# A streaming encoder layer on one core: high and low part of the sample as one stationary operand, squares of the attention's norm split in two, ten attention rows instead of eight

## The chip, the core and the metric

The kernel runs on one core of a Trainium2 chip. The metric is device time in microseconds, the median of several executions; smaller is better. The core has a matrix engine (TensorE, PE in the profile, its weight loads PEld), three engines for elementwise work (DVE = VectorE, ACT = ScalarE, POOL = GpSimd) and a queue that issues all transfers (SP). They run side by side and wait for each other through semaphores.

## What is computed

One layer of an encoder with two branches, for two inputs: a prompt of 2048 frames and a sample of 64 frames that continues a stream of 4096 past frames. All is float32. Cut to what matters:

```
h = rmsnorm(x, norm_g) @ w_in                    # 1024 -> 6144 columns
qa, ka, va, za, qb, kb, vb, zb, ga, gb = split(h)
qa, ka = rmsnorm over 64 (qa, qn_g), (ka, kn_g)
oa = diff_attention(qa, ka, va)                  # (softmax_1 - lam * softmax_2) @ v, 4 heads, v of 128
ob, state = retention(qb, kb, vb)                # 4 heads of 128, with decay
oa = rmsnorm(oa, subln_g) * 0.8 * silu(za)
ob = rmsnorm(ob) * silu(zb)
m  = sigmoid(ga + b0) * (oa @ w_oa) + sigmoid(gb + b1) * (ob @ w_ob)
y  = x + m @ w_out
```

The prompt and the sample share the weights. Outputs are y, k, v and the retention state of both.

## The kernel before

**Split products.** [...] To keep precision, each operand is held as two fp32r parts: a high part (a rounding copy, by ACT) and a low part (the difference, by DVE or POOL). A product of two such operands is three products: high by high, high by low, low by high. In `mm_group` (line 491) these are the three entries of `ops`, with the 128 input features of a step `c` as contraction, 8 steps in all. A product of plain float32 operands, as in `rms_t` (line 812), is one call that the profile shows as two records.

**Projections.** x is normalised, transposed on TensorE and split into `xh`, `xl` (`x_tile`, line 369). Columns of w_in arrive in pieces (`w_load`) and are split on ACT and POOL (`w_split`, `w_piece`, `w_low`). The columns q, k and v of the attention and v of the retention are computed with frames as rows of the result (`natural`, line 587, and `opening`, line 510, for the very first group): x is the stationary operand, 128 frames at a time, and w the moving one, 512 or 256 columns wide. The sample's 64 frames are the ninth tile of half 0 and use 64 stationary columns. After each group of products one of three finishers is spawned (`fin_qk` line 616, `fin_va` line 696, `fin_vb` line 733); it reads the accumulation bank "mm" with ACT and DVE, gives the bank back and stores its results in DRAM scratch. The other columns are computed with w as stationary operand (`transposed`, line 749), where the sample is 64 more moving columns.

**Attention.** For a pair of 128-query blocks `qk_block` (line 926) makes scores in banks "s", DVE moves them out with the position bias into a "row" (128 x 1024 float32), ACT takes exponentials there, and `at_pv` (line 1012) transposes the rows and multiplies by v into the one bank "pv". Of rows there are ROWS = 8 (line 32). `rms_t` (line 794) normalises the result, 33 times in all: squares on ACT, a float32 product by a matrix of 1/128 that sums them over partitions into bank "tp", logarithm and exponential on ACT, a correction step on DVE and POOL.

**Output.** `out_stream` (line 1645) makes, for each of 8 groups of 256 prompt frames (plus 8 sample frames each, 264 columns), 8 tiles of m (`m_tile`, `m_fin`), and from them two tiles of y of 128 frames (`y_tile`, line 1598, and `y_fin`). The sample's columns of m are collected in two tiles `ms`, and its own y tile of 64 rows comes last of all.

**What sets the order.** The kernel writes the instructions of PE, ACT and DVE in a fixed order. A planner does it while the program is built: each stage is a generator (a task with a priority), `loop` (line 86) runs the first task by priority whose wake time has come by PE's estimated clock, and `P`, `A`, `V`, `G` and `ld` (from line 119) add estimated durations. `take` waits for a free buffer of a kind (the numbers are in BUFS, line 33), `give` returns it with a time. So projections, which have the lowest priority, fill the time in which attention waits. On the chip the order is fixed and only semaphores decide the times. All transfers go in order through SP's queue.

## Time and profile before

| | |
|---|---|
| three runs, us | 2001.48, 2004.52, 2001.47; median 2001.48 |
| the profiled execution, us | 2002.83 |
| its span in the trace, us | 2001.0 |
| granted TensorE clock, mean | 0.999 |
| TensorE instructions recorded | 12402 |
| DMA: moved, share of the 16 engines' time | 281 MB, 47.2% on the one queue that carries the data |
| first TensorE product, us from the span's start | 1.05 |

How to read it: the profile is of one execution, with times in microseconds from the start of the span. A line names the source line (L500), the engine, the operation, what it writes and reads by the program's tile names (`mm<-wh,xh`), and its shape; "128\*64" on a product is contraction by stationary columns and "128x512" the moving operand. In brackets stands how long the engine was idle before and what ended that. Names in a pair of read tiles are not in the order of the call. Where tasks interleave, one line of code stands for many groups, so a stage is read by its stretch of time.

### The profile page before, as it was taken

The numbers are of one execution on the slowest core, as the hardware profiler recorded it, in microseconds if no ns is written. First come the engines' busy times: TensorE is split into PE (matmuls) and PEld (weight loads), VectorE is DVE, ScalarE is ACT, GpSimd is POOL, SyncE is SP. The second block draws the span as 40 slices with busy tenths as digits, with TensorE's granted clock in tenths as the row PEclk, the third lists the DMA queues.
The fourth block names the chain that finished last, engine by engine and source line by source line (L and its number), as shares of the span: only waits on it lengthen the run. The fifth ranks groups of instructions, "written<-read, shape, count | busy, mean of one in ns | idle before, by whom it ended". The sixth has DMA issues, their size and how long they took to land.

```text
span 2001.0 us, 34243 instructions
## 1 busy us (share of the span) xinstructions
PE 1985.4 (99%) x12402; PEld 1780.0 (89%) x12402; DVE 992.0 (50%) x2665; ACT 958.6 (48%) x2096; POOL 414.8 (21%) x383
## 2 busy tenths in 40 slices
PE   9999999999999999999999999999999999999999
PEld 7778999999998999999999888888888898889997
DVE  6453666553331421546866555644653457444432
ACT  6432676654442433535766655644654555333330
POOL 2310211211112221221211121221112434222210
PEclk9999999999999999999999999999999999999999
DMA  7646454344565463563353252372233676444431
GB/s 242 202 144 181 131 163 121 105 144 139 158 173 132 136 177 107 160 198 127 110 152 100 75 161 77 106 204 90 74 98 106 203 222 194 152 129 142 135 92 53
DMA packets 330269, 280.96 MB, mean 140 GB/s; under 512 B 64690, under 2 KB 296114, under 8 KB 330099
## 3 DMA queue, kind: packets, MB, share of 16 engines
q1 hardware_dynamic: 330098, 278.77, 47.2%
q8 instruction: 98, 1.61, 0.4%
q14 instruction: 73, 0.59, 0.1%
HBM read 187.19 MB, written 91.49 MB: 139 GB/s over the span
## 4 chain that ended last, share of the span: by engine, by line
PE 95%; DVE 2%; DMA 1%; ACT 1%; issue 0%; SPq 0%; POOL 0%; ACTq 0%; POOLq 0%
PE mm L500 53%; PE s L944 3%; PE s L945 3%; PE at L1624 3%; PE at L1051 3%; PE at L1625 3%; PE at L1626 3%; PE pv L1031 2%; PE pv L1030 2%; PE pv L1029 2%; PE mm L1556 2%; PE mm L1558 2%; PE mm L1557 2%; PE s L1558 2%; PE s L1557 2%; PE s L1556 2%
## 5 line engine op out<-in xcount | busy, mean ns | idle before, releaser
L500 PE MATMUL mm<-xh,wh 128*128 128x512 f32 (+2 forms) x1280 | 461.2, 360 | 0.0
L500 PE MATMUL mm<-xh,wl 128*128 128x512 f32 (+2 forms) x1280 | 451.7, 353 | 0.0
L500 PE MATMUL mm<-xl,wh 128*128 128x512 f32 (+2 forms) x1280 | 450.9, 352 | 0.0
L472 POOL TENSOR_TENSOR wl<-ws,wh 128x512 fp32r<-128x512 f32 x189 | 250.0, 1335 | 906.3 <-ACT wh L462 642.3
L500 PE MATMUL mm<-wh,xh 128*128 128x256 f32 (+3 forms) x864 | 272.1, 315 | 0.5 <-DVE tlo L713 0.3
L500 PEld LDWEIGHTS mm<-xh,wl 128*128 128x128 f32 x1280 | 240.9, 188 | 32.0
L500 PEld LDWEIGHTS mm<-xh,wh 128*128 128x128 f32 x1280 | 241.2, 188 | 29.7 <-issue 0.2
L500 PEld LDWEIGHTS mm<-xl,wh 128*128 128x128 f32 x1280 | 241.4, 189 | 29.0
L500 PE MATMUL mm<-wh,xl 128*128 128x256 f32 (+3 forms) x864 | 266.9, 309 | 0.1
L500 PE MATMUL mm<-wl,xh 128*128 128x256 f32 (+3 forms) x864 | 266.5, 308 | 0.0
L770 ACT COPY ev<-mm 128x512 f32<-128x512 f32 x140 | 71.4, 510 | 241.7 <-PE mm L500 223.1
L500 PEld LDWEIGHTS mm<-wh,xh 128*128 128x128 f32 (+1 forms) x864 | 162.2, 188 | 11.5 <-ACT xh L388 0.6
L500 PEld LDWEIGHTS mm<-wl,xh 128*128 128x128 f32 (+1 forms) x864 | 162.4, 188 | 10.5
L500 PEld LDWEIGHTS mm<-wh,xl 128*128 128x128 f32 (+1 forms) x864 | 162.2, 188 | 10.6 <-DVE xl L389 0.6
L1066 DVE TENSOR_TENSOR atl<-at,ath 128x512 fp32r<-128x512 f32 (+1 forms) x144 | 93.7, 659 | 140.7 <-ACT ath L1064 140.6
L983 ACT ACTIVATE row<-row,a_mx 128x1024 f32<-128x1024 f32 (+7 forms) x160 | 153.5, 963 | 16.6 <-DVE a_mx L963 16.4
L953 DVE CUSTOM_DVE_ANT_0 row<-s,dfar 128x512 f32<-128x512 f32 (+2 forms) x192 | 117.8, 631 | 73.0 <-PE s L945 71.8
L462 ACT CAST wh<-ws 128x512 fp32r<-128x512 f32 x192 | 116.5, 618 | 40.7 <-PE mm L500 28.0
L1064 ACT CAST ath<-at 128x512 fp32r<-128x512 f32 (+1 forms) x144 | 79.5, 563 | 98.9 <-PE at L1051 96.6
L944 PE MATMUL s<-K,q 128*128 128x512 f32 (+3 forms) x320 | 120.2, 381 | 2.5 <-DVE a_acc L953 2.5
L945 PE MATMUL s<-K,q 128*128 128x512 f32 (+3 forms) x320 | 115.4, 362 | 0.0
L1004 DVE SCALAR_TENSOR_TENSOR row<-row,a_w 128x1024 f32<-128x1024 f32 (+4 forms) x96 | 98.1, 1031 | 26.7 <-ACT row L1001 26.5
(207 smaller groups left out, 3943.6 us busy)
## 6 DMA issues: line engine op xcount, KB each, us to landing
ws<-in_w_in_dram SPq DMA_DIRECT2D x192, 256.0 KB, 3.1
q<-qT SPq DMA_DIRECT2D x128, 128.0 KB, 3.0
V<-vN SPq DMA_DIRECT2D x24, 512.0 KB, 5.1
K<-kT SPq DMA_DIRECT2D x48, 256.0 KB, 4.3
gt<-gaT SPq DMA_DIRECT2D x64, 132.0 KB, 2.1
gt<-gbT SPq DMA_DIRECT2D x64, 132.0 KB, 2.2
xt<-in_x_prompt_dram SPq DMA_DIRECT2D x16, 512.0 KB, 6.0
kn<-in_cache_k_T_dram SPq DMA_DIRECT2D x32, 256.0 KB, 4.0
```

The source lines that it names most:

```text
L462: self.nc.scalar.copy(h, st)
L472: self.nc.gpsimd.tensor_sub(l, st, h.bitcast(F32))
L500: nc.tensor.matmul(ps, p, q, start=c == 0 and i == 0, stop=c == KC - 1 and i == 2)
L944: nc.tensor.matmul(ps, q1s, kk, start=True, stop=False)
L945: nc.tensor.matmul(ps, q2s, kk, start=False, stop=True)
L953: nc.vector.tensor_tensor_reduce(out=units[k0 // 1024][:, k0 % 1024:k0 % 1024 + n], in0=ps, in1=tab, scale=-SLOPES[h], scalar=3.0e38, op0= ...
L983: nc.scalar.activation(u, u, AF.Exp, bias=mx, scale=-1.0, accum_out=lp[:, k:k + 1])
L1004: nc.vector.scalar_tensor_tensor(out=u0, in0=u0, scalar=w[:, 0:1], in1=u1, op0=ALU.mult, op1=ALU.add)
L1066: nc.vector.tensor_sub(al[:, :w], at[:, :w], ah[:, :w].bitcast(F32))
L1556: nc.tensor.matmul(ps, wh[:, csl], oh, start=kt == 0, stop=False)
L1557: nc.tensor.matmul(ps, wh[:, csl], ol, start=False, stop=False)
L1558: nc.tensor.matmul(ps, wl[:, csl], oh, start=False, stop=kt == 3)
```

## The change

- The sample's high and low part are copied by GpSimd, when the sample's tile is transposed, into a tile `xs` of 128 columns (64 high, 64 low).
- In `mm_group`, where the result has 64 rows, a step makes two products instead of three: `xs` by the high part of w, into 128 rows of the bank (rows 0 to 63 high by high, rows 64 to 127 low by high), and `xh` by the low part of w, into rows 0 to 63.
- The two halves of the bank then have to be added. `halves` copies all 128 rows out (ACT), a transfer moves rows 64 to 127 to partitions 0 to 63, DVE adds, and the old finisher runs from that buffer instead of from the bank.
- `y_tile` does the same for the sample's y, with `ms` as one tile of 128 columns and `y_halves` as its end. The sample's y tile now stands between the last two prompt tiles, and takes its buffers from the kind "wst" instead of "xt" and "yt".
- In `rms_t`, the copy out of the bank goes first; squares are then taken from the copy, once in float32 and once rounded to fp32r, DVE makes the difference, and the sum over partitions is two fp32r products by the matrix of ones instead of one float32 product.
- ROWS goes from 8 to 10, and the scratch that the program reserves for dynamic DMA is set to 1024 bytes per partition, which makes room.

```diff
-ROWS = 8
+ROWS = 10
@@ x_tile
             self.give(tag, t2)
+            if r == 64:
+                for k, part in enumerate((hi, lo)):
+                    nc.gpsimd.tensor_copy(self.xs[:, 4 * q:4 * q + 4, 64 * k:64 * k + 64], part)
+                    t2 = self.G(256, t2)
@@ mm_group
+            if ps.shape[0] == 64:
+                pair = [(ps, xh, b), (both, self.xs[:, c, :], a)]
+                for i, (o, p, q) in enumerate(pair if c else pair[::-1]):
+                    nc.tensor.matmul(o, p, q, start=c == 0 and i == 0, stop=c == KC - 1 and i == 1)
+                    self.P(n)
+                ops = ()
@@ natural, opening
-            self.spawn(fin(ps[:r, :n * len(group)], r, len(group), t0, self.pe + LAT), 0, "w")
+            self.spawn_fin(fin, ps, r, n * len(group), len(group), t0)
+    def spawn_fin(self, fin, ps, r, n, nu, t0):
+        t = self.pe + LAT
+        done = fin(ps[:r, :n], r, nu, t0, t) if r == 128 else self.halves(ps[:, :n], n, t, fin, t0)
+        self.spawn(done, 0, "w")
+
+    def halves(self, ps, n, t, fin, t0):
+        yield from self.take("ev")
+        up = self.sb(self.ep, [128, 512], "ev", "up")[:, :n]
+        self.nc.scalar.copy(up, ps)
+        t = self.A(n, t)
+        self.give("mm", t)
+        yield t
+        yield from self.take("tlo")
+        dn = self.sb(self.ep, [128, 512], "tlo", "dn")[0:64, :n]
+        t = self.ld(dn, up[64:128], 256 * n)
+        yield t
+        self.nc.vector.tensor_add(up[0:64], up[0:64], dn)
+        t = self.V(n, t)
+        self.give("tlo", t)
+        yield from fin(up[0:64], 64, 1, t0, t, "ev")
@@ rms_t
-        nc.scalar.activation(sq, ps, AF.Square)
-        t1 = self.A(n, t)
         nc.scalar.copy(o, ps)
         t2 = self.A(n, t)
         self.give(tag, t2)
+        nc.scalar.activation(sq, o, AF.Square)
+        self.A(n, t)
+        nc.scalar.activation(hi, o, AF.Square)
+        t1 = self.A(n, t)
         yield t1
+        nc.vector.tensor_sub(lo, sq, hi.bitcast(F32))
+        t = self.V(n, t1)
+        yield t
         yield from self.take("tp")
         mb = self.psum("tp")[:, :n]
-        nc.tensor.matmul(mb, self.ones, sq, start=True, stop=True)
-        t = self.P(4 * n)
+        nc.tensor.matmul(mb, self.ones_r, hi, start=True, stop=False)
+        nc.tensor.matmul(mb, self.ones_r, lo, start=False, stop=True)
+        self.P(n)
+        t = self.P(n)
@@ y_tile
+            if sel is None:
+                pair = [(ps[:64], self.ms[:, ct, 0], wl[:, nsl]), (ps, self.ms[:, ct], wh[:, nsl])]
+                for i, (o, m, w) in enumerate(pair if ct else pair[::-1]):
+                    nc.tensor.matmul(o, m, w, start=ct == 0 and i == 0, stop=ct == 7 and i == 1)
+                    t = self.P(512)
+    def y_halves(self, ps, xt, y, r, t):
+        nc = self.nc
+        yield from self.take("wst")
+        yt = self.sb(self.z4, [128, 512], "wst", "oyt")
+        yield t
+        nc.vector.tensor_copy(yt[64:128], ps[64:128])
+        t2 = self.V(512, t)
+        nc.vector.tensor_add(xt, ps[0:64], xt)
+        t = self.V(512, t)
+        self.give("at", t)
+        yield t2
+        t2 = self.ld(yt[0:64], yt[64:128], 1 << 17)
+        yield t2
+        nc.vector.tensor_add(yt[0:64], yt[0:64], xt)
+        t = self.V(512, max(t, t2))
+        self.give("wst", t)
+        yield t
+        self.give("wst", self.st(y, yt[0:64], 2048 * r))
@@ out_stream
             for tt in range(2):
+                if g == 7 and tt:
+                    yield from self.y_tile(7, None, 64, self.i["x_sample"][0], self.o["y_sample"][0])
...
-        yield from self.y_tile(7, None, 64, self.i["x_sample"][0], self.o["y_sample"][0])
@@ kernel
-    nc = _bacc.Bacc("TRN2", target_bir_lowering=False, num_devices=1)
+    nc = _bacc.Bacc("TRN2", target_bir_lowering=False, num_devices=1, dynamic_dma_scratch_size=1024)
```

More of the change, by code (lines that the diff above doesn't have):

```diff
@@ L29 @@
 NEAR0 = 384
-ROWS = 8
+ROWS = 10
 BUFS = {"thi": 1, "tlo": 2, "ev": 3, "q": 2, "K": 4, "V": 4, "ath": 2, "atl": 2,
-        "ws": 3, "w": 12, "r_o": 1, "r_sq": 1, "r_y": 1, "state": 2,
+        "ws": 3, "w": 12, "r_o": 1, "r_sq": 1, "r_y": 1, "r_hi": 1, "r_lo": 1, "state": 2,
         "mm": 2, "s": 2, "at": 2, "pv": 1, "tp": 1,
@@ L493, in mm_group @@
         seg, xsl = x
+        if ps.shape[0] == 64:
+            both = self.both
         for c in range(KC):
@@ L498, in mm_group @@
             ops = ((a, xh), (a, xl), (b, xh)) if wfirst else ((xh, a), (xh, b), (xl, a))
+            if ps.shape[0] == 64:
+                pair = [(ps, xh, b), (both, self.xs[:, c, :], a)]
[3 more added lines that the diff above has]
+                ops = ()
             for i, (p, q) in enumerate(ops):
@@ L516, in opening @@
         self.x_alloc(1)
+        self.xs = self.xp.tile([128, KC, 128], F32R, tag="xs", name="xs")
         us, low = [], []
@@ L579, in opening @@
             yield from self.take("mm")
-            ps = self.psum("mm")
+            ps = self.both = self.psum("mm")
             self.until(self.xt_ready[j])
@@ L583, in opening @@
                                      j == 8, between)
-            self.spawn(fin(ps[:r], r, 1, 128 * j if j < 8 else T, self.pe + LAT), 0, "w")
+            self.spawn_fin(fin, ps, r, 512, 1, 128 * j if j < 8 else T)
             yield self.pe
@@ L601, in natural @@
                     yield self.xt_ready[j0 + u]
+                self.both = ps[:, :n]
                 yield from self.mm_group(ps[:r, n * u:n * u + n], n, us, slice(0, n),
@@ L619, in fin_qk, with fin @@
         hs = slice(2 * g, 2 * g + nh)
-        def fin(ps, r, nu, t0, t):
+        def fin(ps, r, nu, t0, t, bank="mm"):
             n, ng, rt = 128 * nh * nu, 2 * nh * nu, r * nu
@@ L637, in fin @@
                 t2 = self.V(n, t)
-            self.give("mm", max(t1, t2))
+            self.give(bank, max(t1, t2))
             yield t1
@@ L699, in fin_va, with fin @@
         hs = slice(2 * g, 2 * g + nh)
-        def fin(ps, r, nu, t0, t):
+        def fin(ps, r, nu, t0, t, bank="mm"):
             n, rt = 128 * nh * nu, r * nu
@@ L714, in fin @@
             t3 = self.V(n, t1)
-            self.give("mm", max(t2, t3))
+            self.give(bank, max(t2, t3))
             if t0 < T:
@@ L735, in fin_vb, with fin @@
         ep = self.ep
-        def fin(ps, r, nu, t0, t):
+        def fin(ps, r, nu, t0, t, bank="mm"):
             n, rt = 256 * nu, r * nu
@@ L742, in fin @@
             t = self.A(n, t)
-            self.give("mm", t)
+            self.give(bank, t)
             yield t
@@ L803, in rms_t @@
         o, sq, y = tmp
-        nc.scalar.activation(sq, ps, AF.Square)
-        t1 = self.A(n, t)
+        for k in ("r_hi", "r_lo"):
+            yield from self.take(k)
+        hi, lo = (self.sb(self.tp_, [128, 256], k, None, F32R)[:, :n] for k in ("r_hi", "r_lo"))
         nc.scalar.copy(o, ps)
@@ L808, in rms_t @@
         self.give(tag, t2)
+        nc.scalar.activation(sq, o, AF.Square)
+        self.A(n, t)
+        nc.scalar.activation(hi, o, AF.Square)
+        t1 = self.A(n, t)
         yield t1
+        nc.vector.tensor_sub(lo, sq, hi.bitcast(F32))
+        t = self.V(n, t1)
+        yield t
         yield from self.take("tp")
         mb = self.psum("tp")[:, :n]
-        nc.tensor.matmul(mb, self.ones, sq, start=True, stop=True)
-        t = self.P(4 * n)
+        nc.tensor.matmul(mb, self.ones_r, hi, start=True, stop=False)
+        nc.tensor.matmul(mb, self.ones_r, lo, start=False, stop=True)
+        self.P(n)
+        t = self.P(n)
+        self.give("r_hi", t)
+        self.give("r_lo", t)
         yield t
@@ L1592, in m_fin @@
         yield t2 + 2000
-        for d, m in zip(self.ms, (h, l)):
-            nc.vector.tensor_copy(d[:, ct, 8 * g:8 * g + 8], m[:, 256:GW])
+        for k, m in enumerate((h, l)):
+            nc.vector.tensor_copy(self.ms[:, ct, k, 8 * g:8 * g + 8], m[:, 256:GW])
             t2 = self.V(8)
@@ L1603, in y_tile @@
             nsl = slice(512 * nh, 512 * nh + 512)
-            yield from self.take("xt")
-            xt = self.sb(pb, [128, 512], "xt", "oxt")[:r]
+            tag = "xt" if sel else "wst"
+            yield from self.take(tag)
+            xt = self.sb(pb, [128, 512], tag, "oxt")[:r]
             tx = self.ld(xt, x[:, nsl], 2048 * r)
             yield from self.take("at")
-            run.append((nsl, xt, tx, self.psum("at")[:r]))
+            run.append((nsl, xt, tx, self.psum("at")))
         first = 8 if sel is None else 7
@@ L1614, in y_tile @@
             h, l, t = self.mq[g][ct]
+            wh, wl, tw = self.wout[ct]
             if sel is None:
@@ L1617, in y_tile @@
                 t = max(t, self.msn[-1])
-                h, l = self.ms[0][:, ct, :], self.ms[1][:, ct, :]
+            if max(t, tw[nh]) > self.pe:
+                yield max(t, tw[nh])
+            if sel is None:
[3 more added lines that the diff above has]
+                    t = self.P(512)
             else:
                 h, l = sel(h), sel(l)
-            wh, wl, tw = self.wout[ct]
-            if max(t, tw[nh]) > self.pe:
-                yield max(t, tw[nh])
-            nc.tensor.matmul(ps, h, wh[:, nsl], start=ct == 0, stop=False)
-            nc.tensor.matmul(ps, h, wl[:, nsl], start=False, stop=False)
-            nc.tensor.matmul(ps, l, wh[:, nsl], start=False, stop=ct == 7)
-            for _ in range(3):
-                t = self.P(512)
+                nc.tensor.matmul(ps, h, wh[:, nsl], start=ct == 0, stop=False)
+                nc.tensor.matmul(ps, h, wl[:, nsl], start=False, stop=False)
+                nc.tensor.matmul(ps, l, wh[:, nsl], start=False, stop=ct == 7)
+                for _ in range(3):
+                    t = self.P(512)
             yield self.pe
             if ct == 7:
-                self.spawn(self.y_fin(ps, xt, y[:, nsl], r, max(t, tx)), 0)
+                self.spawn((self.y_fin if r == 128 else self.y_halves)(ps, xt, y[:, nsl], r, max(t, tx)), 0)
+    def y_halves(self, ps, xt, y, r, t):
[16 more added lines that the diff above has]
+        self.give("wst", self.st(y, yt[0:64], 2048 * r))
     def y_fin(self, ps, xt, y, r, t):
@@ L1716, in w_stream @@
         self.z4 = self.es.enter_context(self.tc.tile_pool(name="p3b", bufs=1))
-        self.ms = [self.z4.tile([128, 8, 64], F32R, tag=f"ms{j}", name=f"ms{j}") for j in range(2)]
+        self.ms = self.z4.tile([128, 8, 2, 64], F32R, tag="ms", name="ms")
         self.spawn(self.out_stream(), 8)
@@ L1778, in run @@
             self.xt_ready = []
-            self.ones = self.cp.tile([128, 128], F32, tag="ones", name="ones")
+            self.ones_r = self.cp.tile([128, 128], F32R, tag="ones", name="ones")
+            self.ones = self.ones_r.bitcast(F32)
             nc.vector.memset(self.ones, 1.0 / 128.0)
```

## The prediction, made before the changed kernel ran

> **What bounds the kernel now.** The page's busy times come first, then the shares of the chain that ended last.

> ```profile
> span 2001.0 us, 34243 instructions
> PE 1985.4 (99%) x12402; PEld 1780.0 (89%) x12402; DVE 992.0 (50%) x2665; ACT 958.6 (48%) x2096; POOL 414.8 (21%) x383
> PE 95%; DVE 2%; DMA 1%; ACT 1%; issue 0%; SPq 0%; POOL 0%; ACTq 0%; POOLq 0%
> ```

> TensorE is busy for all but 15.6 us of the span, and 95% of the chain is TensorE's own instructions. DVE and ACT work half the time. An average can hide a stage with another limit, so the second view is busy time by stage. The columns are: stage, length, then busy time and count for PE, weight loads, DVE, ACT and POOL, granted clock, DMA share and GB/s.

> ```profile
> 64.50:190.00 125.50, 124.45 (x622) 99.69 (x621) 60.35 (x147) 41.65 (x101) 17.86 (x14) 1.00 0.55 164
> 190.00:560.00 370.00, 370.00 (x2490) 343.77 (x2489) 197.42 (x606) 209.97 (x472) 64.66 (x55) 1.00 0.50 142
> 560.00:800.00 240.00, 238.18 (x1571) 218.82 (x1571) 57.02 (x153) 83.11 (x203) 47.95 (x38) 1.00 0.52 143
> 800.00:1000.00 200.00, 196.09 (x1554) 190.70 (x1553) 124.38 (x320) 107.63 (x229) 39.91 (x30) 1.00 0.48 148
> 1000.00:1512.00 512.00, 512.00 (x3006) 452.17 (x3005) 294.22 (x786) 299.18 (x578) 92.12 (x72) 1.00 0.38 112
> 1512.00:1620.00 108.00, 108.00 (x550) 91.68 (x549) 38.34 (x78) 48.28 (x118) 37.37 (x38) 1.00 0.55 166
> 1620.00:1985.00 365.00, 364.32 (x2287) 327.75 (x2286) 177.55 (x479) 128.98 (x314) 96.84 (x120) 1.00 0.47 143
> ```

> Both long attention stages (190 to 560 and 1000 to 1512) have no PE idle at all. Between 64.5 and 1985 us it is 1.05 + 1.82 + 3.91 + 0.68 = 7.5 us; the rest of the 15.6 us is the head and the tail. So the kernel costs what its TensorE instructions cost, and a product that goes away should shorten the span by the distance from its start to the next start. (A single record is longer than that distance, because records overlap: starts are what I read below.)

> **The change part by part.** *Projections of the sample.* Before, each of 8 steps makes three products with 64 stationary columns. The change makes two: one with 128 columns (high and low part side by side) and one with 64. Five column groups run this way, three 512 wide and two 256 wide. The length of such a group, from the window that holds just the first wide one, and from the starts of the first narrow one:

> ```profile
> 64.72:70.20 5.48, 5.48 (x25) 1.00 0.77 292
> ```

> ```profile
> 202.09 0.28 PE L500 MATMUL mm<-wh,xh 128*64 128x256 f32 x1
> ...
> 204.82 0.28 PE L500 MATMUL mm<-wh,xh 128*128 128x256 f32 x1
> 204.94 0.28 PE L500 MATMUL mm<-wl,xh 128*128 128x256 f32 x1
> ```

> A wide group is 24 products in 5.48 us, 0.228 each (the 25th record is a neighbour at the edge); a third of it goes: 1.83 us, three times 5.48. A narrow group is 24 products in 204.82 - 202.09 = 2.73 us, 0.114 each; a third is 0.91, two groups 1.82. Products with 128 columns start 204.94 - 204.82 = 0.12 apart, so 16 products of the new kind are 0.1 dearer in all: 1.72. Together **7.2 us**.

> The weight loads speak here, since the new product needs twice the columns. Minimum, median and longest load in ns:

> ```profile
> L500 PEld LDWEIGHTS mm<-xh,wl x1280: 187/188/193, 247.9 to 1617.3; 128*128 128x128 f32 x183
> L500 PEld LDWEIGHTS mm<-wh,xh x864: 133/192/193, 19.0 to 1075.2; 128*128 128x128 f32 x165, 128*64 128x64 f32 x8
> ```

> A 128-column load is recorded at 188 ns and a 64-column one at 133, yet 256-wide products with 128 columns start every 0.12 us. Loads overlap, and I charge them nothing. [...]

> *Output of the sample.* The last 48 products run from 1985.69 to 1996.55, and a last one takes some 0.23 us (1511.57 - 1511.34, two fences below). They become 32:

> ```profile
> 1984.95 1.39 DVE L1638 TENSOR_TENSOR oyt<-at,oxt 128x512 f32<-128x512 f32 x2 [10.09 <-PE at L1626]
> ...
> 1985.21 0.40 PE L1626 MATMUL at<-woh,ml 128*128 128x512 f32 x1
> ...
> 1985.69 0.44 PE L1624 MATMUL at<-woh,ms 128*64 128x512 f32 x1
> ...
> 1996.55 0.40 PE L1626 MATMUL at<-woh,ms 128*64 128x512 f32 x1
> 1996.98 0.68 DVE L1638 TENSOR_TENSOR oyt<-at,oxt 64x512 f32<-64x512 f32 x1 [4.84 <-PE at L1626]
> ```

> 1996.55 + 0.23 - 1985.69 = 11.09 us for 48; a third is **3.70 us**.

> *Norm of the attention.* One float32 product by the matrix of ones becomes two in fp32r, 33 times (each of 33 shows as two records). Its cost, and the start-to-start distance of the float32 product with the 512-wide product ahead of it:

> ```profile
> L812 PE MATMUL tp<-r_sq,ones 128*128 128x256 f32 x66 | 19.6, 378 | 0.0
> ```

> ```profile
> 1511.34 0.39 PE L500 MATMUL mm<-xh,wl 128*128 128x512 f32 x1
> 1511.57 0.59 PE L812 MATMUL tp<-r_sq,ones 128*128 128x256 f32 x2
> 1512.00 0.38 PE L1334 MATMUL pv<-rvx,rqk 128*128 128x128 f32 x2
> ```

> 1512.00 - 1511.57 = 0.43 us before; two times the 0.12 of a 256-wide fp32r product with 128 columns = 0.24 after; 33 x 0.19 = **6.3 us**. The price outside TensorE, by the neighbours on the same tiles:

> ```profile
> L804 ACT ACTIVATE r_sq<-pv 128x256 f32<-128x256 f32 x33 | 12.6, 381 | 22.8 <-PE pv L1031 21.1 <-PE pv L1181 1.3
> L806 ACT COPY r_o<-pv 128x256 f32<-128x256 f32 x33 | 12.2, 369 | 0.7 <-DMA oaT<-r_o 0.7
> L822 DVE SCALAR_TENSOR_TENSOR r_sq<-tp,r_sq 128x256 f32<-128x256 f32 x33 | 13.7, 415 | 8.1 <-ACT r_sq L817 8.0
> ```

> One more Square (0.38) and one subtraction (0.42) per norm: 13 us of ACT and 14 us of DVE over the run, on engines with half their time free. The sum of squares comes 0.37 + 0.38 + 0.42 = 1.2 us later, since the copy now goes first; the bank "pv" comes free 0.38 earlier for the same reason. The cover is the other stream: projections and scores stand between in PE's order. The subtraction makes DVE wait for ACT, with score evictions queued behind it. Such a wait exists already: line 822 waits 8.0 us in all for ACT, and PE idles 0.00 in both attention stages. I take zero; the upper bound is a rival.

> *New evacuation of the sample's groups.* A copy of 128 rows (ACT), a 128 or 64 KB transfer that moves 64 partitions over, an addition (DVE), then the old steps: five times. The accumulation bank is released by the copy alone, earlier than before. What comes later is the sample's k, q and v, which sample attention needs hundreds of us on. Two more buffers are held for that time ("ev" of 3, "tlo" of 2). If a copy had to wait for an "ev", the bank would be held, and the cover is the other bank's group, 5.48 us; the stores that free an "ev" are of the 256 KB kind whose row, further down, has 2.7 us to landing. Zero, with 3 us as upper bound (one such landing uncovered).

> *Copies of the sample's parts on GpSimd.* Four, at the first sample group:

> ```profile
> 58.69 3.79 POOL L472 TENSOR_TENSOR wl<-ws,wh 128x512 fp32r<-128x512 f32 x3 [3.59 <-ACT wh L462]
> 68.47 3.80 POOL L472 TENSOR_TENSOR wl<-ws,wh 128x512 fp32r<-128x512 f32 x3 [5.99 <-ACT wh L462]
> 62.45 0.41 DVE L389 TENSOR_TENSOR xl<-pv,xh 128x256 fp32r<-128x256 f32 x1
> L1428 POOL TENSOR_TENSOR w_o_diffl<-wst,w_o_diffh 128x256 fp32r<-128x256 f32 x6 | 4.4, 740 | 23.7 <-ACT w_o_diffh L1425 15.5 <-DMA wst<-in_w_o_diff_dram 8.2
> ```

> POOL is free at 62.48, the last low part is written at 62.86. By the nearest row, a 256-element subtraction of 0.74 us, the first pair is done at 63.96, the group starts at 64.72 (the window above); the second pair is done at 65.4 and needed four steps on, at 66.5. Zero; at double the price 0.8 us. The next low parts on POOL begin at 68.47 in the old run, so nothing queues behind.

> *Ten rows instead of eight*, from DMA scratch that shrinks. Attention may run further ahead of its softmax. The built order has every other TensorE form in the old number, and attention ends earlier against the projections, which then run alone for longer; the stage where they already do (1512 to 1620) has no idle, so a shift into it costs nothing. It can close or open some of the 7.5 us of idle: half of it either way, 3.8 us, is my bound; I take zero. The page's DMA queues are "hardware_dynamic" and "instruction" only, so I charge the smaller scratch nothing.

> *The end.* The sample's output now stands between the last two prompt tiles. Before, PE stops 0.25 us at a tile's start for the first of two additions (1985.21 + 0.23 to 1985.69); a prompt tile behind the sample finds its bank free: -0.25. The last addition ends as before: 1984.95 + 1.39 = 1986.34 is 1.13 after the last product's start, and 1996.98 + 0.68 = 1997.66 is 1.11 after. But two stores of 256 KB instead of one 128 KB end the run:

> ```profile
> out_y_prompt_dram<-oyt SPq DMA_DIRECT2D x32, 256.0 KB, 2.7
> out_y_sample_dram<-oyt SPq DMA_DIRECT2D x2, 128.0 KB, 2.3
> ```

> That is +0.4, up to +1.0 if they share engines; I take +0.5.

> **The sum:** 7.2 + 3.7 + 6.3 = 17.2, less 0.5, plus 0.25: 16.9 us. The profiled execution took 2002.83 (span 2001.0): 1985.9. The median of the three runs was 2001.48, 1.35 below it: **1984.6 us**.

> **The rivals.**
> *Part is given back* (late "ev", late squares, new gaps from the new order): 3 + 3.8 us and more on top, 1991 to 1997. For it: the 800 to 1000 stage idles 3.91 us, so the written order can miss. Against: idle of 0.00 through the attention stages. Chance 0.08.
> *Gaps close as well* thanks to the two rows: under 1980. Chance 0.04.
> [...] Chance 0.03.
> *Slower, by the norm's chain*: DVE's new subtraction stands in order before score evictions. If each norm found a softmax exponential of 0.96 us in front of its second Square on ACT, and PE ran out of score banks for as long, the price is 33 x 0.96 = 31.7 and the time 1984.6 + 31.7 = 2016. It decides from 17.2 / 33 = 0.52 us of PE stall per norm. The row of the exponential:

> ```profile
> L983 ACT ACTIVATE row<-row,a_mx 128x1024 f32<-128x1024 f32 (+7 forms) x160 | 153.5, 963 | 16.6 <-DVE a_mx L963 16.4
> ```

> Against it: the similar wait of line 822 costs PE nothing. Chance 0.05.

> **How the numbers follow.** The forecast, with its unknowns (+3, +0.8, +3.8, -3.8, not all at once), runs from 1980 to 1991: chance 0.80, and that is the range. A measurement of this kernel tells about 0.2%, 4 us, from no change. Faster: 0.80 + 0.08 + 0.04 = 0.92; same 0.03; slower 0.05.

> **What would show it.** Right: PE busy down by about 17 us to 1968 with idle still near 16; sample groups of 16 products in 3.65 us; the two products of the norm in 0.24; the attention stages without idle. Wrong: PE idle above 20 us, before score products waiting for DVE or before a sample group waiting for POOL; starts of 128-column products wider than 0.23.

## The result, and the profile after

The changed kernel takes **1996.42 us** (median of seven runs, 1995.85 to 1998.74) against 2003.23 for the kernel before on the same chip (seven runs, 2001.47 to 2005.44): ratio 0.9968, 95% interval 0.9958 to 0.9978. It is faster by 0.2 to 0.4%, and the prediction said 1984.6 us with a range from 1980 to 1991. Of 16.9 us expected some 6 to 7 came.

The page of the changed kernel (its profiled execution took 1996.90 us):

```profile
span 1995.0 us, 34222 instructions
PE 1973.8 (99%) x12346; PEld 1773.4 (89%) x12346; DVE 1004.1 (50%) x2707; ACT 972.9 (49%) x2134; POOL 413.3 (21%) x387
PE 89%; DMA 3%; DVE 3%; issue 2%; POOL 1%; ACT 1%; SPq 0%; POOLq 0%; ACTq 0%
```

PE busy fell by 11.6 us and not by 17; PE idle rose from 15.6 to 1995.0 - 1973.8 = 21.2 us; and TensorE's share of the chain fell from 95 to 89%, with DMA, DVE and others in its place. The prediction had named "idle above 20 us" as the sign of being wrong. By stage (columns as in the prediction):

```profile
64.50:190.00 125.50, 120.75 (x602) 99.30 (x601) 63.17 (x149) 43.02 (x104) 18.62 (x14) 0.99 0.55 160
190.00:560.00 370.00, 368.63 (x2452) 342.27 (x2451) 192.60 (x606) 212.42 (x483) 66.08 (x56) 1.00 0.50 141
560.00:800.00 240.00, 239.84 (x1618) 221.44 (x1617) 71.69 (x183) 91.41 (x220) 47.68 (x37) 1.00 0.56 153
800.00:1000.00 200.00, 196.18 (x1556) 191.69 (x1556) 126.39 (x325) 110.84 (x233) 37.41 (x30) 0.99 0.47 147
1000.00:1512.00 512.00, 508.88 (x3025) 449.50 (x3024) 299.31 (x811) 304.84 (x597) 92.90 (x75) 1.00 0.39 112
```

Idle in these five rows: 4.75, 1.37, 0.16, 3.82 and 3.12 us. The two attention stages had none before and have 4.5 together now; the first stage went from 1.05 to 4.75.

**The products went as forecast.** The first wide sample group, and the first and last product of the sample's output:

```profile
63.82:67.47 3.65, 3.65 (x17) 2.39 (x15) 0.59 (x1) 1.70 (x4) 0.03 (x1) 1.00 0.69 258
```

```profile
1972.39 0.50 PE L1673 MATMUL at<-woh,ms 128*128 128x512 f32 x1
...
1979.63 0.39 PE L1673 MATMUL at<-woh,ms 128*128 128x512 f32 x1
```

16 products (and a neighbour at the edge) take 3.65 us instead of 5.48. The output takes 1979.63 + 0.23 - 1972.39 = 7.47 us instead of 11.09. To see the whole, I take the distance from each product's start to the next start, and its median over all 17 traces of this case for products of the same tiles and shape with the same neighbours before and behind. The sum of the medians is the product time, and what the distances are longer is loss (stops, and windows at a lower clock). Before: 1977.1 + 18.4 us. After: 1960.8 + 28.9 us. So **16.3 us of products went, and 10.5 us came back as loss.** With kinds told apart by written tile and size alone it is 14.1 and 8.3, so the split is good to about 2 us.

**Where the loss is.** The two longest single waits of TensorE (total us, times, longest):

```profile
PE tp L703 <- DVE raw L688: 5.2, 4, 4.0
...
PE tp L703 <- ACT wh L466: 1.9, 1, 1.9
```

The stops over 0.9 us behind the head, as distances over their median: 4.2 at 83 us, 0.9 at 487, 2.0 at 991, 1.1 at 1224, 1.0 at 1258, 1.6 at 1487. In the kernel before they were 1.1 at 81, 1.2 at 571, 0.9 at 714 and 1.8 at 957. The longest, on TensorE:

```profile
82.69 0.39 PE L512 MATMUL mm<-wh,xl 128*128 128x512 f32 x1
87.09 0.66 PE L703 MATMUL tp<-ident,raw 128*128 128x128 f32 x4 [4.01 <-DVE raw L688]
...
89.42 0.63 PE L512 MATMUL mm<-wh,xh 128*128 128x512 f32 x1
89.85 0.63 PE L512 MATMUL mm<-wl,xh 128*128 128x512 f32 x1
```

The product at 87.09 transposes normalised k of the first prompt tile. After the stop, products start 0.43 apart instead of 0.23. The granted clock (last but two of the columns) shows why, here and after the second longest stop:

```profile
87.50:91.90 4.40, 4.40 (x15) 3.48 (x14) 2.50 (x8) 1.50 (x4) 0.00 (x0) 0.61 0.73 228
```

```profile
992.50:997.00 4.50, 4.14 (x22) 4.17 (x23) 3.81 (x10) 3.40 (x6) 1.27 (x1) 0.62 0.56 169
```

In the trace's clock record each is a stretch of 3.41 us at half speed, worth 1.7 us. The kernel before has one as well, in its head (0.72 of the clock granted from 10 to 16 us), where the changed one has none.

The 4 us at 83 lie behind the new evacuation. The copy out of the bank (L633) runs on ACT from 68.29 us on; then, on ACT, SP, DVE and GpSimd:

```profile
75.77 0.62 ACT L745 CAST thi<-up 64x512 fp32r<-64x512 f32 x1 [3.60 <-DVE up L641]
77.34 0.59 ACT L665 ACTIVATE sq<-mm 128x512 f32<-128x512 f32 x1
```

```profile
70.44 0.50 SPq L136 DMA_DIRECT2D dn<-up  x1
```

```profile
75.05 0.68 DVE L641 TENSOR_TENSOR up<-up,dn 64x512 f32<-64x512 f32 x1 [7.48 <-DMA dn<-up]
...
78.93 1.21 DVE L205 CUSTOM_DVE_ANT_0 lrow<-lrow 128x64 f32<-128x64 f32 x1
...
83.66 1.23 DVE L233 SCALAR_TENSOR_TENSOR sm_t<-sm_y 128x8 f32<-128x8 f32 x1
84.92 1.19 DVE L234 TENSOR_TENSOR sm_t<-sm_t,ms 128x8 f32<-128x8 f32 x1
86.14 0.17 DVE L235 SCALAR_TENSOR_TENSOR sm_y<-sm_t,sm_y 128x8 f32<-128x8 f32 x1
86.34 0.69 DVE L688 TENSOR_TENSOR raw<-raw,sm_y 128x512 f32<-128x512 f32 x1
```

```profile
77.51 2.54 POOL L476 TENSOR_TENSOR wl<-ws,wh 128x512 fp32r<-128x512 f32 x2 [3.97 <-ACT wh L466]
83.60 2.48 POOL L476 TENSOR_TENSOR wl<-ws,wh 128x512 fp32r<-128x512 f32 x2 [3.55 <-ACT wh L466]
```

Two things are to be seen. The addition (L641) waits for its transfer until 75.05; ACT's L745 waits for the addition, and the squares of the k tile (L665 at 77.34) stand behind L745 in ACT's order. And two instructions over 8 columns take 1.23 and 1.19 us, a third of the same size 0.17: the slow ones lie under GpSimd's subtraction. So does L205 at 78.93, with 1.21 us where a run further down (low_zero_held) has 0.23; the sum of the squares stands behind it in DVE's order. What runs beside an instruction thus sets times too, and not semaphores alone. The stop at 991 is alike: the profile puts it down to ACT's `wh`, but the product reads what DVE's L688 wrote until 992.71, behind L233, L234 and L235 with 1.26, 0.66 and 1.20 us instead of 0.17.

Over the whole run each DVE instruction that is more than 0.15 us longer than the shortest of its kind and shape (kinds that occur at least four times) overlaps a running GpSimd instruction: 115 of 115, with 72.7 us in excess. In the kernel before it is 119 of 119 and 76.7 us, so this is not new. What is new must be where it falls.

### The profile page after: what moved, and what is told of

The parts are those of the page before. It is cut to its first block, busy times and chain, and to the rows that moved or that the text cites. A ratio compares the mean times of both kernels' runs of the same rounds, so it can differ in the third digit from the quotient of the medians.

```text
span 1995.0 us, 34222 instructions
## 1 busy us (share of the span) xinstructions
PE 1973.8 (99%) x12346; PEld 1773.4 (89%) x12346; DVE 1004.1 (50%) x2707; ACT 972.9 (49%) x2134; POOL 413.3 (21%) x387
## 4 chain that ended last, share of the span: by engine, by line
PE 89%; DMA 3%; DVE 3%; issue 2%; POOL 1%; ACT 1%; SPq 0%; POOLq 0%; ACTq 0%
PE mm L512 51%; PE s L992 3%; PE s L993 3%; PE at L1099 3%; PE at L1677 2%; PE at L1678 2%; PE at L1679 2%; PE pv L1079 2%; PE pv L1078 2%; PE pv L1077 2%; PE mm L1604 1%; PE s L1606 1%; PE s L1604 1%; PE s L1605 1%; PE mm L1605 1%
## 5 line engine op out<-in xcount | busy, mean ns | idle before, releaser
L512 PEld LDWEIGHTS mm<-xh,wh 128*128 128x128 f32 x1280 | 241.4, 189 | 28.9 <-issue 0.2
L512 PE MATMUL mm<-wh,xh 128*128 128x256 f32 (+1 forms) x824 | 259.4, 315 | 1.2 <-ACT xh L388 0.5
L512 PE MATMUL mm<-wh,xl 128*128 128x256 f32 (+1 forms) x824 | 254.2, 308 | 0.1
L512 PE MATMUL mm<-wl,xh 128*128 128x256 f32 (+1 forms) x824 | 254.1, 308 | 0.0
L806 ACT COPY ev<-mm 128x512 f32<-128x512 f32 x140 | 71.4, 510 | 214.6 <-PE mm L512 181.2
L512 PEld LDWEIGHTS mm<-wh,xh 128*128 128x128 f32 x824 | 157.9, 192 | 11.0 <-ACT xh L388 0.9
L512 PEld LDWEIGHTS mm<-wl,xh 128*128 128x128 f32 x824 | 158.0, 192 | 8.4
L512 PEld LDWEIGHTS mm<-wh,xl 128*128 128x128 f32 x824 | 157.8, 192 | 8.5 <-DVE xl L389 0.6
L1031 ACT ACTIVATE row<-row,a_mx 128x1024 f32<-128x1024 f32 (+7 forms) x160 | 153.3, 961 | 15.6 <-DVE a_mx L1011 15.6
## 6 DMA issues: line engine op xcount, KB each, us to landing
ws<-in_w_in_dram SPq DMA_DIRECT2D x192, 256.0 KB, 3.1
q<-qT SPq DMA_DIRECT2D x128, 128.0 KB, 3.3
K<-kT SPq DMA_DIRECT2D x48, 256.0 KB, 4.1
kn<-in_cache_k_T_dram SPq DMA_DIRECT2D x32, 256.0 KB, 3.9
```

Of the source, the lines that this page charges most:

```text
L512: nc.tensor.matmul(ps, p, q, start=c == 0 and i == 0, stop=c == KC - 1 and i == 2)
L806: nc.scalar.copy(ev, ps)
L1031: nc.scalar.activation(u, u, AF.Exp, bias=mx, scale=-1.0, accum_out=lp[:, k:k + 1])
```

## The experiments

Two explanations for the loss stood against each other: *the new evacuation* (its wait for a transfer holds up what is queued behind it), and *the order under contention* (a new written order puts DVE instructions that GpSimd stretches where TensorE waits for them). Each expectation names its own theories. The ratios are to the kernel before, beside which each ran; 95% intervals in brackets.

**1. The wait of the addition.** Three ways to move or remove it. `late_add`: the planner reckons 2.5 us more for the transfer, so the addition is written later.

```
-        t = self.ld(dn, up[64:128], 256 * n)
+        t = self.ld(dn, up[64:128], 256 * n) + 2500
```

> The changed kernel, with one number of the planner altered: it reckons 2.5 us more for the transfer that brings the sample's lower half over, so the addition and what follows stand later in the orders of DVE and ACT. Theory A (DVE and ACT wait in order for that transfer, the first k tile's steps queue behind, and PE stops 4.0 us at 82.7 us and then runs a window at half clock): the stop shrinks to about the 0.9 us of the kernel before, the clock stays whole there, and the time falls by 4 to 5 us, to about 1991.5 beside 2003. Theory B (the loss is scattered: any other order of the instructions brings its own small stops): no change beyond 2 us, about 1996. Theory C (the norm's longer chain costs it): no change, 1996.

Measured: 1996.87 us, ratio 0.9963 [0.9949, 0.9976]. The stop at 82 us shrank from 4.2 to 2.4, one of 1.3 us came at 135, and the stretch at half clock stayed (products 0.43 apart from 86.04 to 88.18). What took the wait's place, on DVE and TensorE:

```profile
76.10 1.82 DVE L641 TENSOR_TENSOR up<-up,dn 64x512 f32<-64x512 f32 x1
...
81.50 1.20 DVE L235 SCALAR_TENSOR_TENSOR sm_y<-sm_t,sm_y 128x8 f32<-128x8 f32 x1
82.74 1.71 DVE L688 TENSOR_TENSOR raw<-raw,sm_y 128x512 f32<-128x512 f32 x1
```

The addition waits for nothing now, but it and two more instructions are stretched (0.68, 0.17 and 0.69 us in the fence above of the changed kernel). My expectation of a gain fell.

`first_whole`: only the very first sample group makes three products and uses the old finisher, which pays 1.83 us of products back.

```
-        if ps.shape[0] == 64:
-            both = self.both
+        split = ps.shape[0] == 64 and self.both is not None
@@ opening
+            self.both = None
-            self.spawn_fin(fin, ps, r, 512, 1, 128 * j if j < 8 else T)
+            self.spawn(fin(ps[:r], r, 1, 128 * j if j < 8 else T, self.pe + LAT), 0, "w")
```

> The changed kernel, but the very first sample group (values of the attention) makes its three products per step as before and is finished straight from the bank; the other four groups are split. It pays 8 products, 1.83 us, back. Theory A: the stop at 82.7 us goes, about 5 us with its slow clock, so about 3 us faster than the changed kernel, 1993. Theory B or C: 1.8 us slower than it, 1998.

Measured: 1992.32 us, 0.9947 [0.9932, 0.9962]; the stop at 83 is gone. Without the evacuation at this one place the kernel is 4.1 us faster than the changed one, products included.

`no_wait` keeps every order and takes the transfer out of the addition's operands; the sum of the two halves is left out, and the transfer still runs.

```
-        self.nc.vector.tensor_add(up[0:64], up[0:64], dn)
+        self.nc.vector.tensor_add(up[0:64], up[0:64], up[0:64])
```

> The changed kernel in its own order of instructions, but the addition of the sample's two halves in the projections adds the upper half to itself, so that it waits for no transfer (the transfers still run; the sum of the halves is left out). Theory A (the wait for the transfer is what stops PE at 82.7 us): the stop there falls from 4.2 us to about 1, no half-speed window follows, time 4 to 6 us lower, 1990 to 1992. Rival: the copy in front, ACT's order and the DVE instructions stretched under GpSimd make the stop: it stays at 3 us or more and the time at 1995 or above.

Measured: 1992.23 us, 0.9944 [0.9929, 0.9959]. The stop at 83 is 1.5 us and no stretch at half clock follows; the stops from 987 us on are all there, the first without half clock behind it in this trace. What is left of it, on DVE, with the same two instructions stretched, and on TensorE:

```profile
81.98 1.26 DVE L233 SCALAR_TENSOR_TENSOR sm_t<-sm_y 128x8 f32<-128x8 f32 x1
83.27 1.21 DVE L234 TENSOR_TENSOR sm_t<-sm_t,ms 128x8 f32<-128x8 f32 x1
```

```profile
85.46 0.66 PE L703 MATMUL tp<-ident,raw 128*128 128x128 f32 x4 [1.31 <-DVE raw L688]
```

So the wait is worth about 4 us, the half clock behind it included, and it is not the whole loss.

**2. Parts alone.** `rows_only` is the kernel before with ten rows and the smaller scratch, `norm_only` the kernel before with the new norm, `rows8` the changed kernel with eight rows, `no_norm` the changed kernel with the old norm.

```
rows_only:  -ROWS = 8   +ROWS = 10      (before; and the scratch of 1024 bytes)
rows8:      -ROWS = 10  +ROWS = 8       (changed)
norm_only:  rms_t of the changed kernel in the kernel before
no_norm:    rms_t of the kernel before in the changed kernel
```

> The kernel before with ten rows and the smaller DMA scratch, nothing else. No product goes. Theory A: within 2 us of the kernel before. Theory B: it brings new small stops, 2 to 5 us slower than before, 2005 to 2008.

> The kernel before with the new norm alone (and the smaller DMA scratch), eight rows. By the starts 33 times 0.19: 6.3 us faster, ratio 0.9969. Theory C: same as before or slower. Theory B: 6.3 us less whatever the new order brings, anything from 2 to 8 us faster.

> The changed kernel with 8 attention rows instead of 10. Theory A: rows have no part in it, 1996 within 2 us, and the stop at 82.7 us stays. Theory B in the form that the ten rows rearranged the attention and so made the new stops at 459, 487, 1224, 1258 and 1487 us: those go, 3 to 5 us faster, about 1992.

> The changed kernel with the old norm: one float32 product, squares straight from the bank. If the two fp32r products save what their starts say, 33 times 0.19 us, it is 6.3 us slower than the changed kernel, 2002.7. Theory C (the later squares stall PE and eat the gain): it is as fast as the changed kernel or faster, 1996 or below.

Measured: rows_only 2002.82 us, 1.0004 [0.9994, 1.0013]; norm_only 1999.51, 0.9991 [0.9981, 1.0001]; rows8 1995.27, 0.9959 [0.9945, 0.9974]; no_norm 1998.01, 0.9977 [0.9968, 0.9986]. The rows alone do nothing. The new norm alone takes 6.3 us of products away (1977.1 to 1970.8, medians as above), and of that some 2 us reach the time, if any: a new stop of 3.0 us stands at 953, with half clock behind it. In no_norm 5.5 us of products come back, and the time is 1.6 us longer. In rows8 the stops at 991, 1224, 1258 and 1487 are gone, and 3.0 and 1.1 us at 950 and 954 take their place. On DVE and TensorE of rows8:

```profile
951.51 0.69 DVE L671 TENSOR_TENSOR raw<-mm,gk 128x512 f32<-128x512 f32 x1 [3.97 <-ACT sq L665]
...
953.61 0.38 PE L992 MATMUL s<-K,q 128*128 128x256 f32 x1 [2.81 <-DVE a_acc L1001]
```

Here an evacuation that waits for ACT is written ahead of the score evictions. Each edit gives another written order, and each order has its own stops. A part's effect on the time is its products plus this, and the second is as large as the first.

**3. GpSimd's subtractions.** `low_dve` and `before_low_dve` have all low parts of the weights made on DVE (192 subtractions with 131.7 us of DVE's time in low_dve) in the changed kernel and in the kernel before.

```
-        if n in (5, 7, 8):
+        if True:
             self.nc.vector.tensor_sub(l, st, h.bitcast(F32))
```

> The changed kernel with the low parts of the projection weights (189 subtractions of 1.35 us) made on DVE instead of GpSimd. In both traces every DVE instruction that takes more than 0.15 us over its kind's shortest (119 before, 115 after) runs while GpSimd does. If that stretching is what makes the small stops in the new order (1.14 us instead of 0.16 in the sums of the softmax at 1222 us, 1.14 and 1.20 in the retention's roots at 1486 us), the stops at 1224, 1258 and 1487 go and the time falls by 2 to 5 us. If DVE's own extra 189 times 0.69 = 130 us counts more, it gets slower. Theory A says nothing of this one; its stop at 82.7 us should stay within 1 us.

> The kernel before with the same move of the weights' low parts to DVE. If the stretching costs it stops too (1.6 us at 957 us among them), 1 to 4 us faster than before; if DVE's load counts more, slower.

Measured: low_dve **1985.46 us**, 0.9917 [0.9902, 0.9932], a version with all its work that beats both kernels; before_low_dve 2023.1, 1.0107 [1.0092, 1.0122]. The page of low_dve, and the longest wait of before_low_dve:

```profile
PE 1969.8 (99%) x12346; PEld 1770.4 (89%) x12346; DVE 1068.8 (54%) x2896; ACT 971.8 (49%) x2134; POOL 164.0 (8%) x198
```

```profile
PE s L1556 <- ACT ogh L1513: 13.2, 1, 13.2
```

The excess of DVE fell to 31.8 us, and in low_dve the loss to 18.2. But the edit also gives other orders, and the old kernel's happened to have one wait of 13.2 us. The next runs therefore keep the orders: GpSimd subtracts 8 columns of each part of a piece and fills the rest with zeros (168 of the 189 pieces are made in two parts of 256 columns, so 16 of 512 are subtracted there). The low part of most weights is left out.

```
-            self.nc.gpsimd.tensor_sub(l, st, h.bitcast(F32))
+            lf, hf = l.bitcast(F32), h.bitcast(F32)
+            self.nc.gpsimd.tensor_sub(l[..., 0:8], st[..., 0:8], hf[..., 0:8])
+            self.nc.gpsimd.memset(lf[..., 8:], 0.0)
```

> The changed kernel in its own order on every engine, but GpSimd writes zeros as low part of the weights instead of subtracting (8 columns are still subtracted, for the wait; the rest of the weights' low part is left out). GpSimd is busy some 0.7 us a piece instead of 1.35. If DVE's stretching under GpSimd makes the small stops at 991, 1224, 1258, 1487 us, these shrink below 0.6 us, and the one at 83 loses about 2 of its 4.2 us; 4 to 8 us faster, 1988 to 1992. If the stops come from the order alone (an engine's instruction that waits in front of the one PE needs), they stay and the time is 1995 to 1997.

> The kernel before with the same zeros as low part of the weights. Its stops under the same suspicion are fewer (1.1 us at 81, 1.8 at 957): 1 to 3 us faster than before if stretching counts, none if not. Beside low_zero it says what the change is worth with less of GpSimd in the way: by the products alone 17 us.

Measured: low_zero 1980.16 us, 0.9888 [0.9872, 0.9905]; before_low_zero 1999.14, 0.9985 [0.9975, 0.9994]. Without the subtractions the change is worth 19.0 us, and the loss is 11.0 us in low_zero beside 13.9 in before_low_zero: what the changed kernel lost beyond the one before is gone. The same edit helps the old kernel by 0.15% and the changed one by 0.8%. But GpSimd also worked for a shorter time (0.79 instead of 1.35 us a piece), and staging buffers came free earlier. Two runs take that away. `low_zero_long` adds a second fill and a second subtraction of 8 columns; `low_zero_held` lets the fills overlap the columns of the subtractions, so that all follow ACT's high part and the buffer is held as long as in the changed kernel (from the end of the high part to GpSimd's last write 1.56 us at the median, beside 1.37).

```
             self.nc.gpsimd.tensor_sub(l[..., 0:8], st[..., 0:8], hf[..., 0:8])
+            self.nc.gpsimd.memset(lf[..., 0:], 0.0)              # held;  16: in long
+            self.nc.gpsimd.memset(lf[..., lf.shape[-1] // 2:], 0.0)
+            self.nc.gpsimd.tensor_sub(l[..., -8:], st[..., -8:], hf[..., -8:])    # 8:16 in long
```

> The changed kernel, in the same written orders, with the low part of most weights left out: GpSimd subtracts 16 of the 512 columns in two pieces, one ahead and one behind two fills with zeros, so that it is busy for some 1.3 to 1.4 us a piece, as long as the whole subtraction (1.35 us) and longer than in the run with zeros before (0.79 us). The staging buffer is released at the end, as in the changed kernel. Theory A (VectorE instructions are held up while GpSimd reads and writes two-operand subtractions, and this turns into stops of TensorE): the fills hold nothing up, so VectorE's excess stays near 30 us and the time stays at 1980 to 1984 us, with no stop above 1 us at 82 us. Rival B (GpSimd's time itself, and the staging buffers that come free later for it): the time goes back to the changed kernel's 1993 to 1997 us and the stop at 82 us is there again.

> As the run with long fills, but the fills now overlap the first subtraction's and the last subtraction's columns, so that GpSimd must work in the order subtraction of 8 columns, fill, half fill, subtraction of 8 columns, all behind ScalarE's high part: the staging buffer is held for some 1.3 us after the high part, as by the changed kernel's one subtraction of 1.35 us. (In the run with long fills the fills went ahead of the high part, and buffers came free about 1 us earlier.) Again the low part of most weights is left out. Theory A (it is the subtractions that hold VectorE up): 1980 to 1984 us, VectorE's excess near 30 us, no stop above 1 us between 129 and 1980 us, and at 82 us a stop of at most 2 us, from the late transfer alone. Rival B (the buffers' times): 1990 to 1997 us with stops of 1 to 2 us back at 990, 1224, 1258 and 1487 us.

Measured: 1981.18 us, 0.9897 [0.9881, 0.9914], and 1981.64, 0.9893 [0.9876, 0.9909]. GpSimd's busy time in low_zero_held, and the place of the long stop, on DVE and TensorE (lines behind the edit have numbers four higher than in the changed kernel):

```profile
PE 1967.7 (99%) x12346; PEld 1772.1 (90%) x12346; DVE 955.4 (48%) x2707; ACT 973.5 (49%) x2134; POOL 405.4 (20%) x954
```

```profile
74.25 0.68 DVE L645 TENSOR_TENSOR up<-up,dn 64x512 f32<-64x512 f32 x1 [7.56 <-DMA dn<-up]
...
81.83 0.17 DVE L233 SCALAR_TENSOR_TENSOR sm_t<-sm_y 128x8 f32<-128x8 f32 x1
82.04 0.17 DVE L234 TENSOR_TENSOR sm_t<-sm_t,ms 128x8 f32<-128x8 f32 x1
```

```profile
83.19 0.66 PE L707 MATMUL tp<-ident,raw 128*128 128x128 f32 x4 [0.42 <-DVE raw L692]
```

GpSimd is busy for 405 us, nearly as long as in the changed kernel (413). The addition still waits 7.56 us for its transfer. But the two short instructions take 0.17 each, and TensorE stops for 0.42 us instead of 4.01. Over the run the excess of DVE is 29.6 us instead of 72.7, and TensorE's loss 13.3 instead of 28.9. **So it is the two-operand subtractions that hold DVE up, and neither GpSimd's length nor the buffers.** Together with no_wait: the stop of 4 us needs both, the late addition and the stretched instructions behind it; with either taken away, 1.5 us or less is left. Losses of single traces can differ by some 3 us for the clock in the head alone: of the five in one written order (the changed kernel, no_wait, low_zero, low_zero_long, low_zero_held) two have no half clock in the head, one has 3.41 us of it and two have 6.83.

One instruction shows it in small: L234 took 1.19 us in the changed kernel at 84.92, under a subtraction, and 0.17 in low_zero_held at 82.04, beside a fill that ran from 82.04 to 82.57.

**4. What is left with low parts on DVE.** `low_dve_no_norm` is low_dve with the old norm, `low_dve_rows8` low_dve with eight rows.

> The version with the weights' low parts on DVE, with the old norm. There the stops were nearly gone. If the norm's two products save 33 times 0.19 us wherever PE does not stop, this is 6 us slower than that version, 1991.5. If the later squares eat the gain (theory C), it is within 2 us of it, 1985.5.

> The changed kernel with all weights' low parts on VectorE and with eight attention rows instead of ten. If the two rows do nothing, as in the two pairs without that move, the time is that of ten rows with low parts on VectorE, 1985.5 us, within 3 us. If the order decides (an order that happens to put an evacuation ahead of score evictions), it is 1988 to 1993 us with a stop of over 2 us that ten rows did not have.

Measured: low_dve_no_norm 1993.55 us, 0.9953 [0.9938, 0.9968], with stops of 4.5 us together around 1624; low_dve_rows8 1994.8, 0.9966 [0.9953, 0.9979]. The longest wait of low_dve_rows8:

```profile
PE s L1604 <- ACT w_o_reth L1473: 7.2, 1, 7.2
```

Two rows fewer, with the same products, cost 9.3 us here by one wait at the start of the output stage and 10.24 us at half clock from 1609.5 on, where the same two rows cost nothing in the other two pairs. low_dve's 1985.5 us is thus one order that came out well; that low parts on DVE are better in general is not shown, and before_low_dve speaks against it.

## Why the prediction was wrong, step by step

- *Projections, 7.2 us, and output, 3.7 us:* right. 3.65 us for a wide group, and 11.09 - 7.47 = 3.6 us for the output. The new products load 128 columns in 188 ns at the median, and the wide group's 16 products still come 0.228 us each (3.65 / 16), as the 24 did before: the loads cost nothing here, as I charged.
- *Norm, 6.3 us:* right. In 16 of 33 places the float32 product is 0.43 us ahead of the next start, as in the one I read. In the other 17, where a product of 256 columns or more follows, it is 0.24, but the rest of its price then stands in the next distance: 0.41 instead of 0.23 for a 512-wide product. Before and after, at such a place:

```profile
1410.08 0.59 PE L812 MATMUL tp<-r_sq,ones 128*128 128x256 f32 x2
1410.33 0.58 PE L500 MATMUL mm<-xh,wh 128*128 128x512 f32 x1
1410.74 0.39 PE L500 MATMUL mm<-xl,wh 128*128 128x512 f32 x1
```

```profile
1285.08 0.28 PE L856 MATMUL tp<-r_hi,ones 128*128 128x256 f32 x1
...
1285.54 0.40 PE L512 MATMUL mm<-xl,wh 128*128 128x512 f32 x1
```

The two distances together fell from 0.66 to 0.46 us. The sums of medians give 6.3 us (norm_only) and 5.6 (low_dve against low_dve_no_norm). Of 17.2 us of products 16.3 came: their price is not what failed.
- *New evacuation, "Zero, with 3 us as upper bound":* **the step that failed first.** I named the accumulation bank and the buffers as what could be late, and the cover for them held. What I did not do is ask what is queued behind the addition, on DVE, and behind the copy that waits for it, on ACT: squares of the next tile. I did ask this for the norm's subtraction. It is worth 4 us in time (no_wait and first_whole), and the loss of first_whole is 24.7 us, 4.2 less than the changed kernel's.
- *The other rivals:* weight loads do not set the pace (a step loads 192 columns before and after, and the wide group fell from 5.48 to 3.65 us), and the norm's chain costs no 0.52 us of stop per norm: norm_only is not slower than before.
- *Ten rows and the new order, "half of it either way, 3.8 us":* **the second.** By difference the other 6.3 of the 10.5 us are its, against a bound of 3.8. The measure was wrong: I bounded what a new order can cost by the idle that the old order had. The changed kernel's stops from 487 us on come to 6.6 us over their medians, beside 1.7 for the clock, and single orders elsewhere cost 7 and 13 us. The trace of before held the reason: DVE instructions stretched by 76.7 us in all. The part under the weights' subtractions cost the old order about 3 us (before_low_zero) and the changed one about 15 (low_zero_held), at the place of the new evacuation and elsewhere. I read DVE as half free and did not look at the spread of single durations.
- *Copies on GpSimd, zero:* right; the first sample group starts at 63.82 without a stop.
- *The end, +0.5:* not seen. From the start of the last product to the end of the span it was 2001.0 - 1996.55 = 4.45 us, and it is 1995.0 - 1990.76 = 4.24 in the changed kernel, whose last product (L1679) starts at 1990.76.
- *The rival "part is given back",* 1991 to 1997 with a chance of 0.08, is what happened, through "new gaps from the new order"; its "late ev" and "late squares" were not what came late. With 0.00 idle in the attention stages as evidence against it, I had taken a property of one written order for a property of the stage. I had also looked for new idle before score products; 2.6 us of it stand there, and 5.2, 1.9 and 1.4 before transposes that wait for DVE.

Open: how the 4.6 us of the transfer (issued at 70.44, addition at 75.05) divide between the weight loads ahead of it on the same queue and those behind was not tried. Nor was an order searched for in which the stretched instructions lie off the path while the low parts stay on GpSimd.

The stops late in the run have the same look. At 1487 us, on DVE, GpSimd and TensorE of the changed kernel:

```profile
1485.86 1.14 DVE L234 TENSOR_TENSOR sm_t<-sm_t,ms 128x4 f32<-128x4 f32 x1
1487.03 1.20 DVE L235 SCALAR_TENSOR_TENSOR sm_y<-sm_t,sm_y 128x4 f32<-128x4 f32 x1
1488.26 0.69 DVE L1420 TENSOR_TENSOR rru<-rru,sm_y 128x512 f32<-128x512 f32 x1
```

```profile
1485.66 1.31 POOL L1344 TENSOR_TENSOR rvx<-rqk,rtab 128x512 f32<-128x512 f32 x1 [2.05 <-DMA rqk<-qbT]
1486.93 1.27 POOL L476 TENSOR_TENSOR wl<-ws,wh 128x512 fp32r<-128x512 f32 x1
```

```profile
1489.00 0.66 PE L1426 MATMUL tp<-ident,rru 128*128 128x128 f32 x4 [1.40 <-DVE rru L1420]
```

Each of the two stretched instructions ends with the GpSimd instruction beside it: 1487.00 and 1486.97, then 1488.23 and 1488.20. Two excesses of about 1 us each are more than the stop of 1.40.

## What to carry to other kernels

Where a bound engine runs in an order that is written when the program is built, a change that removes its work can also give a new order, and here 10.5 of the 16.3 us won came back as loss; measure products and stops apart, and do not take the old order's idle as a bound for the new one's. For each new wait, name what is queued behind it on its own engine and on the engine that waits for it. Look at the spread of single durations as well as at busy shares: two 8-column VectorE instructions that took 1.23 and 1.19 us beside a GpSimd subtraction, instead of 0.17, stood here ahead of what TensorE waited for in its stop of 4.01 us.

## What was not expected of the hardware

```profile
902.00:904.00 2.00, 1.49 (x7) 0.88 (x6) 1.58 (x7) 0.00 (x0) 0.00 (x0) 1.00 0.00 0
904.00:906.00 2.00, 1.42 (x7) 0.78 (x6) 1.58 (x5) 1.63 (x4) 0.00 (x0) 0.99 0.00 0
906.00:910.00 4.00, 4.00 (x17) 3.61 (x18) 2.16 (x10) 2.58 (x6) 0.00 (x0) 0.58 0.22 75
```

A busy share of 0.73 over 4 us, (1.49 + 1.42) / 4, was followed by 0.58 of the clock. The kernel before has the same 1.49 and 1.42 us from 908 to 912, with 1.00 of the clock from 912 to 916, and its stop of 1.8 us at 957 has no half clock behind it either (1.00 granted from 955 to 965). So one stop's length alone does not decide it here; what else the granted clock goes by was not measured.
